# Copies of x in the places of late weights, an earlier DMA transpose of the third step's x, and stores placed behind a transpose

## The chip, the cores and the metric

The kernel runs on one core of one Trainium2 chip. The metric is the device time in microseconds (us) of that core.

TensorE is called PE in the views, VectorE DVE, ScalarE ACT, GpSimd POOL, SyncE SP. POOL issues the loads; SP issues stores and DMA transposes in the order of the program. Some words of the text: a transfer *lands* when its data are there and whoever waits for it may go on; the *chain* is the work that ended last, followed back step by step to what released it; an *eviction* is ACT's copy of a finished result out of PSUM; a *seed* is ACT's copy of a start value into the PSUM bank in which a part of a node is then summed; *dts* is a copy of one more sum of the node, from which DVE subtracts; *half clock* is a stretch in which the profile grants PE 0.50 of its clock.

## The reference

A causal convolution over time with eight taps, each a 512x512 matrix, on 8 sequences of 4096 steps.

```python
out = np.zeros_like(x)                       # x: [8, 4096, 512] float32
for k in range(8):
    shifted = x if k == 0 else np.concatenate([np.zeros((B, k, D)), x[:, :-k]], axis=1)
    out += np.matmul(shifted, kernel[k])     # kernel: [8, 512, 512]
```

## The kernel before

The kernel saves products with a Karatsuba-like scheme of three levels: for each pair of halves (LO, HI) of eight times and eight taps it also makes a middle one (MID), from sums of x and differences of weights. The sequence is cut into steps `i` of eight times for each of 128 partitions. A step has three nodes, LO, HI and MID, of nine products each (the very first node has 16 direct ones instead); a product is four matmuls of 128x512. The order of nodes is `(0,LO) (1,LO) (0,HI) (1,HI) (0,MID) (1,MID)`, then MID, LO, HI for each later step. Here "the second step" is `i = 1`, "the third" `i = 2`; node 6 is the first node of the third step. Up to node 6 every operation is placed by hand; from node 6 on there is a loop.

```python
def transpose_x(i, h):                       # DMA transpose, on SP
    nc.sync.dma_start_transpose(out=XT[:, 4*h:4*h+4, :]..., in_=xin[i, h]...)

def prep_m():                                # sums for the MID node of a step, on DVE
    tt(D1[:, 0:2], XT[:, 7::-7], XT[:, 0:2], ADD)
    tt(pairs(D2[:, 1:5]), pairs(XT)[:, 3::-3], pairs(XT)[:, 0:2], ADD)

def node_e(n, b_):                           # cut: nodes 4 and 5
    for a in (LO, HI):
        y = first[n.i, a, b_]
        tt(y, y, p, ADD if a == LO else SUB)
        store(n.i, a, b_, y)                 # on SP
...
# hand-placed part, around the second step's MID node (other lines cut)
tt(D1[:, 1], XT[:, 0], XT[:, 1], ADD)        # these sums read XT[0:4] of step 1
tt(D1[:, 0], X0[:, 1], XT[:, 0], ADD)
tt(D2[:, 1:3], X0, XT[:, 0:2], ADD)
tt(D2[:, 3:5], XT[:, 0:2], XT[:, 2:4], ADD)
node_u(nodes[5])                             # a product of XT[0] of step 1
prep_d21()
transpose_x(2, 0)                            # overwrites XT[0:4]
...
prep_m()                                     # first use of the third step's x
...
transpose_x(2, 1)                            # overwrites XT[4:8]
...
prep_d4(HI)                                  # the last sum before the loop
for k, (i, a) in enumerate(order):           # k >= 6
    if a == MID and more:
        transpose_x(i + 1, 0)                # for k == 6: "the third transpose"
```

`XT` is one buffer of eight times. A transpose of the next step can start only when every reader of the old contents is through. Below, `transpose_x(2, 0)` is the lower transpose, `transpose_x(2, 1)` the upper one and `transpose_x(3, 0)` the third.

## Time and profile before

| | before |
|---|---|
| median of the three runs known at the prediction | 787.44 us |
| span of the profiled run (its time: 786.55 us) | 784.4 us |
| PE, DVE, ACT busy | 98%, 84%, 36% |
| last sum before the loop ends | 88.3 us |
| node 8's first product of its last part starts | 100.75 us |

A line of a timeline has the start in us, the time taken, the engine, the line of the program, the operation, what it writes and reads, and how often it was repeated without a break. The bracket at its end is the idle time of the engine just before it, with what ended it. A loss "start to start" is the start of a line minus that of the line above, minus the number of matmuls in the line above times 0.2155 us.

The prediction shows PE and the chain. The timeline of DVE for the same hand-over, the stretch from about 68 to 101 us in which PE passes from the second step to the third, has three lines that matter:

```profile
69.43 0.70 DVE L76 TENSOR_TENSOR pp<-dts,pp 128x512 f32<-128x512 f32 x1 [0.82 <-ACT dts L276]
...
72.70 2.96 DVE L76 TENSOR_TENSOR D<-XT 128x1024 bf16<-128x1024 bf16 x3 [1.90 <-DMA XT<-xin]
...
87.09 1.23 DVE L76 TENSOR_TENSOR D<-XT 128x2048 bf16<-128x2048 bf16 x1 [0.50 <-DMA XT<-xin]
```

An engine that is behind with its list sits idle 0.82 + 1.90 + 0.50 = 3.2 us, 2.4 of them behind transposes. The line at 87.09 is the last sum, for which the third transpose must wait.

### The profile page before, as it was taken

The numbers are of one execution on the slowest core, as the hardware profiler recorded it, in microseconds if no ns is written. First come the engines' busy times: TensorE is split into PE (matmuls) and PEld (weight loads), VectorE is DVE, ScalarE is ACT, GpSimd is POOL, SyncE is SP. The second block draws the span as 40 slices with busy tenths as digits, with TensorE's granted clock in tenths as the row PEclk, the third lists the DMA queues.
The fourth block names the chain that finished last, engine by engine and source line by source line (L and its number), as shares of the span: only waits on it lengthen the run. The fifth ranks groups of instructions, "written<-read, shape, count | busy, mean of one in ns | idle before, by whom it ended". The sixth has DMA issues, their size and how long they took to land.

```text
span 784.4 us, 9508 instructions
## 1 busy us (share of the span) xinstructions
PE 767.3 (98%) x3620; PEld 349.0 (44%) x3620; DVE 659.3 (84%) x762; ACT 281.2 (36%) x458; POOL 42.8 (5%) x83
## 2 busy tenths in 40 slices
PE   7899999999999999999999999999999999999997
PEld 4444344444444444444444444444444444444443
DVE  3998898988888988888988888888888898888895
ACT  2363333233333333333333333333333333333332
POOL 5000000000000000000000000000000000000000
PEclk9999999999999999999999999999999999999999
DMA  9944987778778677978776888777778787788753
GB/s 164 210 76 118 259 187 164 190 174 170 191 185 197 163 183 167 190 177 206 165 192 162 172 195 198 171 178 173 175 172 204 186 169 179 166 177 199 177 154 125
DMA packets 159229, 138.37 MB, mean 176 GB/s; under 512 B 130130, under 2 KB 134226, under 8 KB 159184
## 3 DMA queue, kind: packets, MB, share of 16 engines
q1 hardware_dynamic: 145312, 98.84, 45.8%
q0 software_dynamic: 13728, 38.66, 30.6%
q8 instruction: 28, 0.46, 0.2%
q10 hardware_dynamic: 144, 0.26, 0.1%
q14 instruction: 17, 0.14, 0.1%
HBM read 77.32 MB, written 67.11 MB: 184 GB/s over the span
## 4 chain that ended last, share of the span: by engine, by line
PE 92%; DMA 5%; DVE 1%; POOL 1%; issue 0%; ACT 0%; DVEq 0%; SPq 0%; POOLq 0%
PE pp L214 91%; DMA XT<-xin 3%; DMA xin<-in_x_dram 2%; DVE D L76 1%; POOL w L80 0%; DVE y L76 0%; PE pp L191 0%; ACT XT L390 0%; POOL D L80 0%; DVE pp L76 0%; DVEq L629 0%; ACT pp L270 0%; POOL xin L80 0%; DVE f L76 0%; POOL identn L148 0%
## 5 line engine op out<-in xcount | busy, mean ns | idle before, releaser
L214 PE MATMUL pp<-w,D 128*128 128x512 bf16 x3304 | 721.6, 379 | 6.3 <-DVE pp L76 1.8
L214 PEld LDWEIGHTS <-D 128*128 128x128 bf16 x3304 | 322.6, 98 | 398.3 <-DVE D L76 5.4
L76 DVE TENSOR_TENSOR D<-D 128x1024 bf16<-128x1024 bf16 (+2 forms) x251 | 228.3, 949 | 0.1
L76 DVE TENSOR_TENSOR y<-pp,ms 128x1024 f32<-128x1024 f32 (+1 forms) x121 | 146.4, 1212 | 44.6 <-PE pp L214 44.5
L76 DVE TENSOR_TENSOR D<-XT 128x2048 bf16<-128x2048 bf16 (+2 forms) x155 | 143.4, 942 | 16.1 <-DMA XT<-xin 14.8
L258 ACT COPY pp<-pp 128x512 f32<-128x512 f32 x95 | 54.1, 570 | 261.5 <-PE pp L214 261.5
L270 ACT COPY pp<-pp 128x512 f32<-128x512 f32 x95 | 54.1, 570 | 170.6 <-PE pp L214 168.1
L76 DVE TENSOR_TENSOR pp<-dts,pp 128x512 f32<-128x512 f32 x95 | 65.6, 691 | 43.8 <-ACT dts L276 42.6
L314 ACT COPY ms<-pp 128x1024 f32<-128x1024 f32 x60 | 61.0, 1016 | 34.0 <-PE pp L214 34.0
L80 POOL DMA_DIRECT2D xin<-in_x_dram x64 | 34.0, 532 | 694.5 <-DMA XT<-xin 679.1
L286 DVE SCALAR_TENSOR_TENSOR pp<-pp,dts 128x512 f32<-128x512 f32 x95 | 66.0, 694 | 3.2
L276 ACT COPY dts<-pp 128x512 f32<-128x512 f32 x95 | 57.4, 604 | 2.0 <-PE pp L214 2.0
L272 ACT ACTIVATE pp<-pp 128x512 f32<-128x512 f32 x95 | 56.0, 589 | 1.9 <-DVE f L76 1.7
L214 PE MATMUL pp<-w,XT 128*128 128x512 bf16 x124 | 31.8, 379 | 0.0
L76 DVE TENSOR_TENSOR w<-w,w 128x2048 bf16<-128x2048 bf16 x19 | 22.6, 1217 | 3.2 <-DMA w<-in_kernel_dram 3.0
L214 PEld LDWEIGHTS <-XT 128*128 128x128 bf16 x124 | 12.1, 98 | 14.6
L185 PE MATMUL pp<-zero,ident 128*128 128x512 bf16 x20 | 6.6, 484 | 3.1 <-POOL ident masks.py:199 3.1
L214 PE MATMUL pp<-w,w 128*128 128x512 bf16 x36 | 8.6, 379 | 0.0
L356 DVE CAST D<-pp 128x1024 bf16<-128x1024 f32 x1 | 1.2, 1224 | 7.1 <-PE pp L202 7.1
L80 POOL DMA_DIRECT2D w<-in_kernel_dram x8 | 6.0, 768 | 1.9 <-DMA w<-in_kernel_dram 1.8
L191 PE MATMUL pp<-ident,xin 128*128 128x128 bf16 x48 | 3.2, 219 | 2.3 <-DMA xin<-in_x_dram 2.1
L214 PEld LDWEIGHTS <-w 128*128 128x128 bf16 x36 | 3.4, 98 | 3.8
(50 smaller groups left out, 68.7 us busy)
## 6 DMA issues: line engine op xcount, KB each, us to landing
out_dram<-y SPq DMA_DIRECT2D x123, 512.0 KB, 3.5
xin<-in_x_dram POOLq DMA_DIRECT2D x64, 512.0 KB, 5.7
w<-in_kernel_dram POOLq DMA_DIRECT2D x8, 512.0 KB, 16.5
out_dram<-ms SPq DMA_DIRECT2D x2, 512.0 KB, 3.3
out_dram<-f SPq DMA_DIRECT2D x2, 512.0 KB, 4.1
XT<-xin SPq DMA_TRANSPOSE x61, 6.2
D<-in_x_dram POOLq DMA_DIRECT2D x1, 508.0 KB, 5.5
D<-in_x_dram POOLq DMA_DIRECT2D x1, 381.0 KB, 7.0
```

The source lines that it names most:

```text
L76: nc.vector.tensor_tensor(out=o, in0=a, in1=b, op=op)
L80: nc.gpsimd.dma_start(out=out, in_=src)
L185: nc.tensor.matmul(pw[:, h], lhsT=ident, rhs=zero, start=True, stop=True)
L191: nc.tensor.transpose(o[:, t - t0, c * P:(c + 1) * P], src[:, t, c * P:(c + 1) * P], ident)
L214: nc.tensor.matmul(bank, lhsT=comp[:, c * P:(c + 1) * P], rhs=w[:, c, :], start=start and c == 0, stop=c == DC - 1, skip_group_check=True)
L258: nc.scalar.copy(out=n.q[:, 0], in_=n.q[:, 1])
L270: nc.scalar.copy(out=n.p[b_][:, 1], in_=n.q[:, 1])
L272: nc.scalar.mul(out=n.p[b_][:, 1], in_=n.q[:, 1], mul=-1.0)
L276: nc.scalar.copy(out=n.dts, in_=n.q[:, 0])
L286: nc.vector.scalar_tensor_tensor(out=p[:, 0], in0=p[:, 1], scalar=-1.0, in1=n.dts, op0=MUL, op1=SUB)
L314: nc.scalar.copy(out=ms[b_], in_=p)
L356: nc.vector.tensor_copy(out=D4[:, 0:2], in_=bank["d4a"])
```

## The change

Two places of weights that are filled late, `W[MID,HI,MID]` and `W[MID,LO,MID]`, hold copies of x until then: C1 the second step's first four times, C0 the first step's last two, which X0 held before. A tile of zeros takes a copy of one time (U1). The second step's middle sums A1 and D21 read the copies (F21 is made from D21), so the lower transpose can run long before. Moreover the additions of nodes 4 and 5 are parted from their stores, the stores come later (five of eight behind the upper transpose), and the whole hand-placed part, its start too, is in a new order. The diff, cut to its core:

```diff
-    X0 = spool.tile([P, 2, D], bf, name="X0")
+    A1 = spool.tile([P, 2, D], bf, name="A1")
+    U1 = zero
+        if (i, a) == (1, MID):
+            return (U1, [A1[:, 0], A1[:, 1]], [D21[:, 0], D21[:, 2]],
+                    [F21[:, j] for j in range(4)])
+    def node_y(n, b_, a):                    # addition without its store
+        y = first[n.i, a, b_]
+        tt(y, y, n.p[b_], ADD if a == LO else SUB)
+    C0, C1 = W[MID, HI, MID], W[MID, LO, MID]
# start: w4 first, transposes of H ahead, w6 before w5, another order of products
+    nc.scalar.copy(out=C0[:, 0:2], in_=XT[:, 6:8])
+    nc.scalar.copy(out=C1, in_=XT[:, 0:4])
# node 2
+    node_seed(nodes[2], 0)
+    nc.scalar.copy(out=U1, in_=XT[:, 0])
+    node_dts(nodes[2])
+    tt(A1[:, 0], C0[:, 1], C1[:, 0], ADD)
+    transpose_x(2, 0)
# nodes 3 and 4
+    tt(D21[:, 2:4], C1[:, 0:2], C1[:, 2:4], ADD)
+    tt(D21[:, 0:2], C0[:, 0:2], C1[:, 0:2], ADD)
+    tt(A1[:, 1], C1[:, 0], C1[:, 1], ADD)
+    prep_m()                                 # was ahead of node 5's last part
# nodes 5 and 6
+    prep_d4(LO)
+    store(0, LO, 1, first[0, LO, 1])
+    transpose_x(2, 1)
+    store(0, HI, 1, first[0, HI, 1])
+    node_y(nodes[5], 1, LO)                  # the tile ms
+    store(1, LO, 1, first[1, LO, 1])
```

More of the change, by code (lines that the diff above doesn't have):

```diff
@@ L306, in node_e @@
             first[n.i, n.a, b_] = y
-        elif n.k < 6:
-            for a in (LO, HI):
-                y = first[n.i, a, b_]
-                tt(y, y, p, ADD if a == LO else SUB)
-                store(n.i, a, b_, y)
         elif n.a == MID:
@@ L340, in direct @@
                 W[LO, n >> 1, n & 1], m == 0)
-    def add(y, p, op):
-        tt(y, y, p, op)
+    C0, C1 = W[MID, HI, MID], W[MID, LO, MID]
+    load_w(4)
+    transpose_pe("xh", 2, H, 5, 8)
+    sums_pe("d4a", 1, (-4, 0), (-3, 1))
     load(H[1:P, 1:4], xr[0:P - 1, RUN - 7:RUN - 4, :])
-    sums_pe("d4a", 0, (-4, 0), (-3, 1))
-    sums_pe("d4b", 3, (-2, 2), (-1, 3))
+    load_w(6)
+    sums_pe("d4b", 2, (-2, 2), (-1, 3))
+    nc.vector.tensor_copy(out=XF[:, 0:3], in_=bank["xh"])
     transpose_pe("xf", 2, xin[0, 0], 0, 4)
+    load_w(5)
@@ L353 @@
+    nc.vector.tensor_copy(out=D4[:, 0:2], in_=bank["d4a"])
     nc.scalar.copy(out=D4[:, 2:4], in_=bank["d4b"])
-    load_w(4)
     n0.p = {0: pair(0), 1: pair(1)}
-    nc.vector.tensor_copy(out=D4[:, 0:2], in_=bank["d4a"])
-    nc.scalar.copy(out=XF[:, 3:7], in_=bank["xf"])
-    transpose_pe("xh", 0, H, 5, 8)
-    direct(0, 2)
-    load_w(5)
-    load_w(6)
-    load_w(7)
-    load_x(0, 1)
-    direct(0, 3)
+    fill(pair(3))
+    load_w(7)
+    direct(0, 2)
+    direct(0, 1)
+    direct(0, 3)
@@ L365 @@
+    nc.scalar.copy(out=XF[:, 3:7], in_=bank["xf"])
     sums_pe("e4a", 2, (-5, -1), (-6, -2))
-    direct(0, 1)
-    nc.vector.tensor_copy(out=XF[:, 0:3], in_=bank["xh"])
     nc.vector.memset(XF[:, 0:3, 0:D:G], 0.0)
-    load_x(1, 0)
     tt(D2, XF[:, 0:5], XF[:, 2:7], ADD)
+    direct(2, 3)
+    tt(F21, D2[:, 0:4], D2[:, 1:5], ADD)
+    mid_dve(1, LO, HI)
+    sums_pe("e4b", 2, (-7, -3))
     direct(1, 2)
     direct(0, 0)
-    sums_pe("e4b", 2, (-7, -3))
-    tt(F21, D2[:, 0:4], D2[:, 1:5], ADD)
@@ L375 @@
-    mid_dve(1, LO, HI)
+    load_x(0, 1)
     tt(D1, XF[:, 2:4], XF[:, 3:5], ADD)
-    load_w(2)
+    mid_dve(2, LO, HI)
+    nc.scalar.copy(out=E4[:, 3:1:-1], in_=bank["e4a"])
+    mid_dve(2, LO, LO)
+    load_x(1, 0)
+    load_w(0)
     nc.vector.tensor_copy(out=E4[:, 1], in_=bank["e4b"][:, 0])
-    fill(pair(3))
-    mid_dve(1, LO, LO)
     direct(1, 3)
-    nc.scalar.copy(out=E4[:, 3:1:-1], in_=bank["e4a"])
-    nc.scalar.copy(out=F0, in_=XF[:, 3])
-    direct(2, 1)
-    mid_dve(2, LO, LO)
@@ L386 @@
-    mid_dve(2, LO, MID)
     direct(1, 1)
     transpose_pe("x1", 2, xin[0, 1], 0, 4)
-    mid_dve(2, LO, HI)
     nc.scalar.copy(out=XT[:, 4:8], in_=bank["x1"])
+    load_w(2)
+    mid_dve(1, LO, LO)
+    direct(1, 0)
+    transpose_pe("x2", 2, xin[1, 0], 0, 4)
+    mid_dve(2, LO, MID)
+    load_w(1)
+    tt(D4[:, 4:8], XF[:, 3:7], XT[:, 4:8], ADD)
+    direct(2, 1)
+    nc.vector.tensor_copy(out=XT[:, 2:4], in_=bank["x2"][:, 2:4])
+    prep_d42(HI)
+    nc.scalar.copy(out=XT[:, 0:2], in_=bank["x2"][:, 0:2])
@@ L391 @@
+    nc.scalar.copy(out=C0[:, 0:2], in_=XT[:, 6:8])
+    tt(T4, XT[:, 4:8], XT[:, 0:4], ADD)
     direct(3, 1)
-    tt(D4[:, 4:8], XF[:, 3:7], XT[:, 4:8], ADD)
-    direct(2, 3)
-    transpose_pe("x2", 2, xin[1, 0], 0, 4)
-    nc.scalar.copy(out=X0, in_=XT[:, 6:8])
+    prep_d41(HI)
+    tt(T42[:, 0:2], D4[:, 6:8], T4[:, 0:2], ADD)
+    direct(3, 0)
+    nc.scalar.copy(out=C1, in_=XT[:, 0:4])
     direct(2, 0)
-    nc.scalar.copy(out=XT[:, 0:2], in_=bank["x2"][:, 0:2])
-    prep_d42(HI)
-    direct(1, 0)
@@ L400 @@
-    direct(3, 0)
-    nc.vector.tensor_copy(out=XT[:, 2:4], in_=bank["x2"][:, 2:4])
-    tt(T4, XT[:, 4:8], XT[:, 0:4], ADD)
-    load_w(0)
-    load_w(1)
+    nc.scalar.copy(out=F0, in_=XF[:, 3])
     direct(3, 3)
+    fill(pair(2))
     tt(D41[:, 1], T4[:, 0], T4[:, 1], ADD)
-    fill(pair(2))
+    load_w(3)
+    tt(T42[:, 2:4], T4[:, 0:2], T4[:, 2:4], ADD)
     node_a1(1)
-    load_w(3)
-    tt(D41[:, 0], D4[:, 7], T4[:, 0], ADD)
-    mid_dve(1, HI, HI)
     direct(2, 2)
     node_e(nodes[0], 0)
+    tt(D41[:, 0], D4[:, 7], T4[:, 0], ADD)
@@ L414 @@
     node_a0(nodes[1])
+    node_u(nodes[1])
+    direct(3, 2)
+    mid_dve(1, HI, HI)
+    node_seed(nodes[1], 0)
     prep_d27()
-    node_u(nodes[1])
-    tt(T42[:, 2:4], T4[:, 0:2], T4[:, 2:4], ADD)
-    direct(3, 2)
-    tt(T42[:, 0:2], D4[:, 6:8], T4[:, 0:2], ADD)
+    node_dts(nodes[1])
+    node_seed(nodes[1], 1)
+    tt(D42[:, 3], D4[:, 1], D4[:, 3], ADD)
+    node_v(nodes[1], 0)
+    tt(D421[:, 0], D42[:, 7], T42[:, 0], ADD)
     load_x(1, 1)
-    tt(D42[:, 3], D4[:, 1], D4[:, 3], ADD)
@@ L422 @@
-    prep_d41(HI)
-    node_seed(nodes[1], 0)
+    node_v(nodes[1], 1)
+    tt(D421[:, 1:4], T42[:, 0:3], T42[:, 1:4], ADD)
+    node_a1(2)
+    mid_dve(2, HI, LO)
     transpose_x(1, 1)
-    node_dts(nodes[1])
-    node_v(nodes[1], 0)
-    node_seed(nodes[1], 1)
-    tt(D421[:, 0], D42[:, 7], T42[:, 0], ADD)
-    node_a1(2)
-    tt(D421[:, 1:4], T42[:, 0:3], T42[:, 1:4], ADD)
     mid_dve(1, HI, LO)
-    node_e(nodes[0], 1)
     node_d(nodes[1], 0)
-    node_v(nodes[1], 1)
-    mid_dve(2, HI, LO)
+    node_l(nodes[1], 0, LO)
@@ L436 @@
+    mid_dve(2, HI, MID)
     nc.scalar.copy(out=D4[:, 2:4], in_=T4[:, 2:4])
@@ L438 @@
     load_x(2, 1)
+    node_e(nodes[0], 1)
+    node_u(nodes[2])
     node_l(nodes[1], 0, HI)
-    node_l(nodes[1], 0, LO)
-    mid_dve(2, HI, MID)
     node_e(nodes[1], 0)
+    node_a0(nodes[2])
+    node_seed(nodes[2], 0)
     prep_d421(HI)
-    node_a0(nodes[2])
-    node_u(nodes[2])
+    load_x(2, 0)
     mid_dve(2, HI, HI)
+    node_l(nodes[1], 1, LO)
+    node_l(nodes[1], 1, HI)
+    nc.scalar.copy(out=U1, in_=XT[:, 0])
+    node_v(nodes[2], 0)
     prep_d4(HI)
-    node_seed(nodes[2], 0)
@@ L449 @@
-    node_l(nodes[1], 1, LO)
+    nc.scalar.copy(out=D42[:, 3], in_=T42[:, 3])
+    node_seed(nodes[2], 1)
+    node_v(nodes[2], 1)
     node_dts(nodes[2])
-    node_v(nodes[2], 0)
+    mid_dve(0, HI, HI)
+    node_e(nodes[1], 1)
+    prep_d41(HI)
     node_d(nodes[2], 0)
-    nc.scalar.copy(out=D42[:, 3], in_=T42[:, 3])
-    prep_d41(HI)
-    node_seed(nodes[2], 1)
-    node_l(nodes[1], 1, HI)
-    node_v(nodes[2], 1)
-    mid_dve(0, HI, HI)
+    node_l(nodes[2], 0, HI)
+    tt(A1[:, 0], C0[:, 1], C1[:, 0], ADD)
@@ L459 @@
+    prep_d42(HI)
     node_d(nodes[2], 1)
-    load_x(2, 0)
+    transpose_x(2, 0)
     mid_dve(0, LO, HI)
-    node_l(nodes[2], 0, HI)
-    node_e(nodes[1], 1)
     node_a1(3)
-    load_x(3, 0)
     node_l(nodes[2], 0, LO)
-    prep_d42(HI)
     node_a0(nodes[3])
     node_e(nodes[2], 0)
+    mid_dve(0, LO, LO)
+    tt(D421[:, 0:4], D42[:, 3:7], D42[:, 4:8], ADD)
     node_u(nodes[3])
+    node_l(nodes[2], 1, HI)
+    node_seed(nodes[3], 1)
+    node_seed(nodes[3], 0)
+    node_dts(nodes[3])
     mid_dve(1, MID, HI)
-    mid_dve(0, LO, LO)
@@ L473 @@
-    node_seed(nodes[3], 0)
-    node_seed(nodes[3], 1)
-    tt(D421[:, 0:4], D42[:, 3:7], D42[:, 4:8], ADD)
-    node_dts(nodes[3])
-    node_l(nodes[2], 1, HI)
+    node_v(nodes[3], 1)
+    node_d(nodes[3], 1)
+    mid_dve(0, HI, LO)
     node_v(nodes[3], 0)
+    node_d(nodes[3], 0)
+    node_l(nodes[2], 1, LO)
     node_a1(4)
-    node_v(nodes[3], 1)
-    node_d(nodes[3], 0)
-    mid_dve(0, HI, LO)
-    node_d(nodes[3], 1)
     mid_dve(1, MID, LO)
-    node_l(nodes[2], 1, LO)
+    tt(D21[:, 2:4], C1[:, 0:2], C1[:, 2:4], ADD)
@@ L486 @@
+    node_l(nodes[3], 1, HI)
+    node_l(nodes[3], 0, LO)
+    mid_dve(2, MID, MID)
+    node_e(nodes[2], 1)
+    load_x(3, 0)
     node_l(nodes[3], 0, HI)
-    node_e(nodes[2], 1)
-    node_l(nodes[3], 0, LO)
-    node_l(nodes[3], 1, LO)
     node_a0(nodes[4])
-    mid_dve(2, MID, MID)
+    tt(D21[:, 0:2], C0[:, 0:2], C1[:, 0:2], ADD)
     node_u(nodes[4])
     node_e(nodes[3], 0)
-    node_l(nodes[3], 1, HI)
+    node_l(nodes[3], 1, LO)
+    tt(A1[:, 1], C1[:, 0], C1[:, 1], ADD)
     mid_dve(2, MID, LO)
+    mid_dve(2, MID, HI)
@@ L496 @@
     node_seed(nodes[4], 0)
+    node_v(nodes[4], 0)
     node_seed(nodes[4], 1)
     node_dts(nodes[4])
-    mid_dve(2, MID, HI)
-    tt(D1[:, 1], XT[:, 0], XT[:, 1], ADD)
-    node_v(nodes[4], 0)
-    node_v(nodes[4], 1)
-    tt(D1[:, 0], X0[:, 1], XT[:, 0], ADD)
     node_d(nodes[4], 0)
     node_a1(5)
-    tt(D2[:, 1:3], X0, XT[:, 0:2], ADD)
+    node_v(nodes[4], 1)
+    prep_m()
+    node_l(nodes[4], 0, HI)
     node_l(nodes[4], 0, LO)
-    node_l(nodes[4], 0, HI)
-    tt(D2[:, 3:5], XT[:, 0:2], XT[:, 2:4], ADD)
@@ L510 @@
-    node_u(nodes[5])
-    node_d(nodes[4], 1)
     node_a0(nodes[5])
     node_e(nodes[3], 1)
+    node_d(nodes[4], 1)
+    node_u(nodes[5])
     node_seed(nodes[5], 0)
-    prep_d21()
+    node_l(nodes[4], 1, LO)
+    tt(F21[:, 0], D2[:, 0], D21[:, 0], ADD)
+    node_l(nodes[4], 1, HI)
+    node_y(nodes[4], 0, LO)
+    node_y(nodes[4], 0, HI)
+    store(0, LO, 0, first[0, LO, 0])
+    tt(F21[:, 1], D21[:, 0], D21[:, 1], ADD)
+    node_dts(nodes[5])
     node_v(nodes[5], 0)
+    prep_d27()
     node_seed(nodes[5], 1)
-    transpose_x(2, 0)
+    store(0, HI, 0, first[0, HI, 0])
@@ L519 @@
+    load_x(3, 1)
+    node_y(nodes[4], 1, LO)
     node_v(nodes[5], 1)
-    node_l(nodes[4], 1, LO)
-    node_e(nodes[4], 0)
-    node_l(nodes[4], 1, HI)
-    node_dts(nodes[5])
-    prep_d27()
     node_d(nodes[5], 0)
     node_d(nodes[5], 1)
-    prep_m()
+    tt(F21[:, 2:4], D21[:, 1:3], D21[:, 2:4], ADD)
     node_l(nodes[5], 0, LO)
@@ L530 @@
     node_a1(6)
+    node_l(nodes[5], 1, HI)
+    node_u(nodes[6])
     prep_d4(LO)
-    node_e(nodes[4], 1)
-    node_l(nodes[5], 1, HI)
+    store(0, LO, 1, first[0, LO, 1])
+    node_y(nodes[4], 1, HI)
     node_a0(nodes[6])
-    node_e(nodes[5], 0)
-    node_u(nodes[6])
+    node_y(nodes[5], 0, LO)
+    prep_d41(LO)
+    transpose_x(2, 1)
     node_l(nodes[5], 1, LO)
-    prep_d41(LO)
-    tt(D21[:, 2:4], D2[:, 2:4], D2[:, 3:5], ADD)
-    node_dts(nodes[6])
-    load_x(3, 1)
-    node_seed(nodes[6], 0)
-    tt(D21[:, 0:2], D2[:, 0:2], D2[:, 1:3], ADD)
-    node_seed(nodes[6], 1)
-    node_v(nodes[6], 0)
-    node_a1(7)
-    node_v(nodes[6], 1)
-    transpose_x(2, 1)
-    node_d(nodes[6], 0)
-    node_e(nodes[5], 1)
-    node_d(nodes[6], 1)
-    prep_d42(LO)
+    store(0, HI, 1, first[0, HI, 1])
+    node_seed(nodes[6], 0)
+    node_v(nodes[6], 0)
+    node_y(nodes[5], 0, HI)
+    tt(D21[:, 0:2], D2[:, 0:2], D2[:, 1:3], ADD)
+    node_dts(nodes[6])
+    node_seed(nodes[6], 1)
+    node_v(nodes[6], 1)
+    tt(D21[:, 2:4], D2[:, 2:4], D2[:, 3:5], ADD)
+    node_d(nodes[6], 0)
+    prep_d42(LO)
+    node_y(nodes[5], 1, HI)
+    node_d(nodes[6], 1)
+    store(1, LO, 0, first[1, LO, 0])
+    node_y(nodes[5], 1, LO)
+    store(1, HI, 0, first[1, HI, 0])
+    node_a1(7)
+    store(1, HI, 1, first[1, HI, 1])
     prep_d4(HI)
+    store(1, LO, 1, first[1, LO, 1])
     for k, (i, a) in enumerate(order):
```

## The prediction

> **What bounds the kernel now.** I read the page first, its table of engines and its chain that ended last.
>
> ```profile
> PE 767.3 (98%) x3620; PEld 349.0 (44%) x3620; DVE 659.3 (84%) x762; ACT 281.2 (36%) x458; POOL 42.8 (5%) x83
> ...
> PE 92%; DMA 5%; DVE 1%; POOL 1%; issue 0%; ACT 0%; DVEq 0%; SPq 0%; POOLq 0%
> ```
>
> TensorE (PE) is busy for 767.3 of 784.4 us, and 92% of the chain is PE. The change leaves every product in place (the same 866 products of four matmuls, the same transposes and fills), so only time in which PE waits can be won. Next, the windows: the stretch 200 to 400 us holds 928 matmuls, so a matmul costs 200/928 = 0.2155 us and a product of four 0.862 us. The kernel's steady part has no gap. The gaps are in the first 100 us, so I read the timeline of PE there.
>
> ```profile
> 22.08 1.03 PE L214 MATMUL pp<-w,D 128*128 128x512 bf16 x4
> 25.17 1.07 PE L191 MATMUL pp<-ident,xin 128*128 128x128 bf16 x16 [2.06 <-DMA xin<-in_x_dram]
> ...
> 68.18 1.89 PE L214 MATMUL pp<-w,D 128*128 128x512 bf16 x8 [0.71 <-ACT pp L270]
> ...
> 78.58 1.02 PE L214 MATMUL pp<-w,D 128*128 128x512 bf16 x4 [0.63 <-ACT pp L270]
> 80.85 8.87 PE L214 MATMUL pp<-w,D 128*128 128x512 bf16 x40 [1.25 <-ACT pp L272]
> 90.17 8.82 PE L214 MATMUL pp<-w,D 128*128 128x512 bf16 x40 [0.46 <-DVE D L76]
> 100.75 2.75 PE L214 MATMUL pp<-w,D 128*128 128x512 bf16 x12 [1.76 <-DVE pp L76]
> ```
>
> The idle in brackets is counted from the modelled end of the last matmul, so it is too small. Start to start it is more: 40 matmuls from 80.85 should take 8.62 us, until 89.47, and the next starts at 90.17: 0.70 lost. In the same way 0.88, 0.10, 0.80, 1.41, 0.70 and 1.96 us are lost at 68.18, 76.05, 78.58, 80.85, 90.17 and 100.75, together **5.85 us in the hand-over from the second step to the third**. Between 29 and 60 us some 0.7 us are lost, at 28.19 0.39, and at 25.17 2.23 in the wait for the second half of the first x. The loop after 100.75 loses nothing.
>
> What ends those late waits is in the chain in order of time: ACT and VectorE (DVE) are only the last links, behind three DMA transposes.
>
> ```profile
> 66.68 6.00 DMA XT<-xin
> 72.67 0.02 issue
> 72.70 2.96 DVE D L76 x3
> ...
> 80.65 6.34 DMA XT<-xin
> ...
> 88.39 8.72 DMA XT<-xin
> 97.11 0.02 issue
> ```
>
> The first transpose (third step, lower half) can start at 66.68 only: XT[0:4] is read until then by the second step's sums D1, D2 and by a product of XT[0]. DVE sits until 72.70. The second one (upper half) waits behind DVE work and a store until 80.65; the third (fourth step, lower half) waits for the last sum of the third step, at 88.3, and the sums behind it at 97.1 feed the product at 100.75. So DVE is late through all of it.
>
> **What the Trainium skill says.** "TensorE: Matmul & The Clock Gate", section "Wait — 56ns, not 53.3ns?", gives 215.7 ns start to start for 512 columns at the full clock; the trace agrees (215.5). "VectorE: DVE Perf Modes", section on the perf-mode tiers, gives 1224 ns for a 2048-element bf16 tensor_tensor; the trace has 1217 as the duration. Back to back such operations start 1.135 us apart here (42.65, 43.79, 44.92), and I count with that. "Perfetto Trace Analysis", on HWDGE instructions, says that an issue's window leaves out the movement of the data: agreed, the issue at 80.65 shows 4.75 us on the SP queue and lands after 6.34. "DMA: Bandwidth & Descriptors", rules for authors, advises to issue a transfer early and wait late. That is what this change does.
>
> **The change, part by part.**
>
> *Copies.* X0 goes (one 1024-element ACT copy, 1.05 us). C0 takes its place (1.05), and C1 (2048 elements, 1.87 by the like copy at 26.27) and U1 (512, 0.62 by the F0 copy) are added on ACT: +2.5 us on an engine that is half idle between 28 and 45 us. In a place where ACT waited for PE 3.8 us (before 34.11) C1 costs nothing. They free XT[0:4] when prep_d4(HI) has read it, by my count at 46 us instead of 66.7. The lower transpose is then bound by its input: that load is issued at 45.15 now, lands in about 5.7, so transpose from about 51 to 57 us, in a stretch where the DMA engines show a share of 0.00. It leaves the path: **prep_m wants it only at about 64**.
>
> *DVE.* Spacings from the DVE timeline: 2048 bf16 1.135 us, 1024 0.60, 512 0.335, a float32 addition of 1024 from PSUM 1.13, a 512 subtraction in PSUM 0.60. The second step's middle sums were 0.335x2 + 0.60x2 + 1.135 = 3.0; they become A1 0.335x2, D21 0.60x2 and F21 0.335x2 + 0.60 = 3.14. All else moves. From 28.15 on I add DVE's list in its new order, to the last sum before the loop: weights' differences done by 63.2, then 21.2 us more, plus some 0.65 of waits where PE delivers late (the y of node 4's second half): **85.0**, against 88.3 before. DVE, not PE, now sets this date.
>
> *PE.* The same 8 direct products stand before the transposes of the second half of x; that half is the eighth or so transfer, and the same bytes lie ahead of it in the queue (order w4, H, w6, w5, w7 instead of H, w4, w5, w6, w7). So it lands at 25.1 as before and the 2.23 us stay, though the first product may come some 0.4 us sooner; that only lengthens this wait. Then one product instead of two lies beside the 1.87 us eviction, 0.86 us more of waiting up to 28.19. From 29.05: 58 products and one fill to the first product of node 6's last part: 58 x 0.862 + 0.43 = 50.4, with some 0.6 of small waits for DVE: 80.1. Before this product started at 82.57. **Won there: 2.5 us.**
>
> *What remains.* In the loop PE would reach node 8's first last-part product at 80.1 + 18 products x 0.862 = 95.6; before it was 100.75. But this product hangs on the third transpose: last sum 85.0, transpose 6.2 (median landing) to 8.7 (its time now), then prep_m, a sum and a subtraction, 3.6 us as now (97.11 to 100.75): 94.9 to 97.4. With a middle value of 7.6 for the transpose it is 96.3, so 0.7 us of the 5.1 stay. Sum: 100.75 - 96.3 = **4.4 us won**, and all later times move by it. 787.44 - 4.4 = 783.0.
>
> *Stores behind transposes.* The adds are split from their stores, and the stores stand later in the SP queue. This frees the transpose of the upper half at about 74 (prep_d4(LO) done) instead of 80.65. It lands near 80.5, before DVE wants it at 84.
>
> **The rivals.**
>
> 1. *A wait of stores takes the place of the transposes.* The tile ms is written again by node 6's eviction on ACT, which must wait for the second step's store. That store now stands behind the upper transpose, whose issue holds SP for some 4.75 us from 74: store at 79.5, landing (3.3 in the table of issues, more behind a transpose) at 83 to 84.7. PE delivers at 82. ACT then seeds node 7 at 84.6 to 86.2, and PE wants that at 84.5: 0 to 1.8 us lost. Against: the product at 96.3 is set by DVE and the third transpose, so a loss here is mostly hidden behind the one already counted. It would make 783 to 784.5.
>
> 2. *DVE is the bound, and nearly all stays.* From 30 to 60 us DVE is busy 9.93, 10.00 and 9.96 of each 10 us. If the new order leaves it a wait (a weight late, the eviction of x), each microsecond goes into the last sum and the third transpose. With 2 us of such waits 785.
>
> 3. *The start moves too.* If the w4-first order and the transposes of H beside the wait for x let everything begin earlier, up to 2.6 us at 25.17 and 28.19 are to be had: 780.5. Against: the DMA share is 1.19 from 10 to 20 us, the queue is saturated, and the awaited transfer has the same bytes ahead of it.
>
> 4. *The transposes were hidden anyway*, and nothing comes of it: 787. Against it are the 5.85 us of counted gaps, which the chain puts behind exactly these transposes.
>
> **Range and chances.** Best: all 5.85 and a little of the start, 781.0. Worst plausible: half of the hand-over regained by DVE waits and stores, 785.6. I put 783.0 in the middle. Faster by over 2% would need 15.7 us; all gaps after the first product are 9.2 us, so next to impossible. Slower by 2% would need a new wait in every step of the loop, and the loop's text is untouched.
>
> **What would show it.** Right: PE's timeline without gaps of over 0.5 us from 30 to 85; the lower transpose issued near 51; no DVE wait for XT near 70; the upper one issued near 74; the third near 85, and one residual gap of 0 to 1.7 us near 96; the first half of x still awaited until about 25. Wrong: x landing well before 24 (rival 3); ACT's ms eviction waiting for a store (rival 1); the last sum before the loop later than 86.5 (rival 2); or new gaps inside the loop after 105, which would mean that the order of x loads shifted against the transposes there.

## The result, and the profile after

Over six runs each, the changed kernel takes 783.22 us in the median (782.97 to 784.06), the kernel before 787.81 (786.40 to 789.12). The ratio is 0.9945, with a 95% interval from 0.9932 to 0.9958. A ratio is the mean time of one kernel's runs over that of the other's of the same rounds, so it is not quite the ratio of the medians. The two profiled spans are 784.4 and 780.9 us, 3.5 us apart.

The page's engines and chain after:

```profile
PE 767.4 (98%) x3620; PEld 349.0 (45%) x3620; DVE 659.3 (84%) x764; ACT 283.2 (36%) x460; POOL 42.8 (5%) x83
...
PE 94%; DMA 3%; DVE 1%; POOL 1%; issue 0%; ACT 0%; DVEq 0%; POOLq 0%
```

Nothing has become less work: PE and DVE are as busy as before, ACT has 2.0 us more. Only the DMA's part of the chain fell, from 5% to 3%. PE's timeline after, at the lines that answer to those in the prediction:

```profile
20.07 3.61 PE L215 MATMUL pp<-w,D 128*128 128x512 bf16 x16 [0.91 <-DMA w<-in_kernel_dram]
25.08 1.07 PE L192 MATMUL pp<-ident,xin 128*128 128x128 bf16 x16 [1.40 <-DMA xin<-in_x_dram]
...
28.10 1.05 PE L192 MATMUL pp<-ident,xin 128*128 128x128 bf16 x16 [1.09 <-ACT XT L390]
...
39.95 8.10 PE L215 MATMUL pp<-w,D 128*128 128x512 bf16 x36
48.79 12.28 PE L215 MATMUL pp<-w,D 128*128 128x512 bf16 x56 [0.74 <-DVE pp L76]
...
70.58 1.89 PE L215 MATMUL pp<-w,D 128*128 128x512 bf16 x8
72.66 1.89 PE L215 MATMUL pp<-w,F 128*128 128x512 bf16 x8 [0.19 <-DVE pp L76]
...
78.71 21.32 PE L215 MATMUL pp<-w,D 128*128 128x512 bf16 x96
99.86 1.03 PE L215 MATMUL pp<-w,XT 128*128 128x512 bf16 x4
```

- The large gaps from 68 to 101 us are gone. Start to start, 0.36 us are lost at 72.66 (70.58 + 8 x 0.2155 = 72.30), 0.46 between 78.71 and 99.86, 0.18 at 63.67: 1.0 us in place of 5.85. **The hand-over won 4.85 us.**
- A new gap stands at 48.79: 39.95 + 36 x 0.2155 = 47.71, so 1.08 us. With two small ones the stretch from 29 to 60 us loses 1.25 us in place of 0.7. **0.55 us are given back.**
- In the start, the second transposes on PE begin at 28.10 in place of 28.19, but one product fewer (0.862) is done by then: **0.77 us given back.** x still arrives at 25.08.

4.85 - 0.55 - 0.77 = 3.53, the difference of the spans. The chain after, in order of time, shows what is left of the hand-over:

```profile
72.66 13.27 PE pp L215 x61
85.93 7.70 DMA XT<-xin
93.63 0.02 issue
93.66 1.01 DVE D L76 x2
```

One transpose is left in this stretch of the chain, the third. DVE's timeline shows where its idle time went:

```profile
64.54 0.69 DVE L76 TENSOR_TENSOR D<-XT 128x1024 bf16<-128x1024 bf16 x1
65.60 1.23 DVE L76 TENSOR_TENSOR D<-XT 128x2048 bf16<-128x2048 bf16 x1 [0.37 <-PE pp L215]
...
84.64 1.22 DVE L76 TENSOR_TENSOR D<-XT 128x2048 bf16<-128x2048 bf16 x1
```

The first two lines are prep_m, which stood at 72.70 before, behind the lower transpose. The third is the last sum, 2.45 us earlier than at 87.09 and without a wait.

### The profile page after: what moved, and what is told of

Its sections match the earlier page's. It is cut to its first block, busy times and chain, and to the rows that moved or that the text cites. A ratio compares the mean times of both kernels' runs of the same rounds, so it can differ in the third digit from the quotient of the medians.

```text
span 780.9 us, 9507 instructions
## 1 busy us (share of the span) xinstructions
PE 767.4 (98%) x3620; PEld 349.0 (45%) x3620; DVE 659.3 (84%) x764; ACT 283.2 (36%) x460; POOL 42.8 (5%) x83
## 3 DMA queue, kind: packets, MB, share of 16 engines
q1 hardware_dynamic: 145312, 98.84, 46.3%
## 4 chain that ended last, share of the span: by engine, by line
PE 94%; DMA 3%; DVE 1%; POOL 1%; issue 0%; ACT 0%; DVEq 0%; POOLq 0%
PE pp L215 94%; DMA xin<-in_x_dram 2%; DMA XT<-xin 1%; POOL w L80 0%; DVE D L76 0%; PE pp L192 0%; DVE pp L76 0%; ACT XT L390 0%; DVE y L76 0%; POOL D L80 0%; DVEq L648 0%; POOL xin L80 0%; POOL identn L148 0%; PE pp L186 0%; POOL ident masks.py:199 0%
## 5 line engine op out<-in xcount | busy, mean ns | idle before, releaser
L76 DVE TENSOR_TENSOR D<-D 128x2048 bf16<-128x2048 bf16 (+2 forms) x250 | 227.2, 948 | 3.4 <-ACT D L369 3.4
L215 PE MATMUL pp<-w,F 128*128 128x512 bf16 x36 | 8.7, 379 | 0.2 <-DVE pp L76 0.2
```

The lines of the kernel that those rows point to most:

```text
L76: nc.vector.tensor_tensor(out=o, in0=a, in1=b, op=op)
L215: nc.tensor.matmul(bank, lhsT=comp[:, c * P:(c + 1) * P], rhs=w[:, c, :], start=start and c == 0, stop=c == DC - 1, skip_group_check=True)
```

## The experiments

In each batch all kernels ran on one chip with runs of the kernel before between them. The changed kernel itself was run again in the second and third batch, so three ratios of it are known: 0.9945, 0.9957 and 0.9949.

### Was it the early transpose? One copy undone

```diff
-            return (U1, [A1[:, 0], A1[:, 1]], ...
+            return (XT[:, 0], [A1[:, 0], A1[:, 1]], ...
-    nc.scalar.copy(out=U1, in_=XT[:, 0])
-    transpose_x(2, 0)                        # node 2
     node_u(nodes[5])
+    transpose_x(2, 0)
     tt(F21[:, 2:4], D21[:, 1:3], D21[:, 2:4], ADD)
+    prep_m()                                 # was in node 4
```

> The changed kernel with one copy undone: the second step's middle stream is read from XT[0] and not from U1, so the lower transpose (third step) must again wait for that product (about 68.8 us), and prep_m follows it, just ahead of node 6. Theory (the gain is the early lower transpose): transpose issued near 69, lands near 75, DVE waits for it about 1 us and does prep_m late, last sum before the loop near 88, product of node 8 near 99.9 instead of 97.3; span up by 2 to 3 us over the changed kernel's 780.9, ratio to before 0.997 to 0.999. Rival (the gain comes from the reordered start and stores, copies only accompany it): span within 1 us of 780.9, ratio 0.994 to 0.996.

Measured: 788.35 us (787.18 to 788.99), ratio 1.0015 (1.0003 to 1.0027), span 786.6. The whole gain is gone and a little more. The direction fits the theory and contradicts the rival; the size does not: the span is 5.7 us above 780.9, twice what was expected. DVE hardly waited for the lower transpose. The last sum came about as expected, started at 86.85 (84.64 in the changed kernel; 0.5 us of that is x landing later in this run). What was not expected is in the chain:

```profile
85.72 1.22 DVE ms L76
86.94 0.02 issue
86.96 10.19 DMA out_dram<-ms
97.15 0.02 issue
97.17 1.02 ACT ms L317
```

The second step's second store of ms took 10.19 us to land, next to the third transpose, which was issued at 88.14 and landed at 99.0, after 10.8 us (7.7 in the changed kernel). ACT's eviction into ms waited for it, and PE for ACT: 1.79 us are lost start to start at 98.84. The first store of ms did the same a little earlier. It stands behind the upper transpose, whose issue held SP for 5.93 us from 77.17 (1.70 in the changed kernel), so it went out at 83.77 only; ACT waited 3.39 us for it, until 87.74, and PE lost 1.46 us at 89.29. That is the prediction's rival 1, here as it was written. The cause of the long issue and the long landings stays open. A load of x issued shortly before was my suspicion, since this kernel's loads wait for its transposes (74.44 and 85.74, against 55.59 and 79.78 in the changed one); but where the upper transpose here, issued 2.7 us behind such a load, took 8.0 us to land, that of the stores-only kernel below, issued 2.5 us behind one, took 4.7.

### Was it the early sums? prep_m alone moved back

```diff
     node_v(nodes[4], 1)
-    prep_m()
     tt(F21[:, 2:4], D21[:, 1:3], D21[:, 2:4], ADD)
+    prep_m()
```

> The changed kernel with only the third step's first sums (prep_m, 1.74 us of DVE) moved back from node 4 to just ahead of node 6's first product; copies, early lower transpose and all else as changed. Theory (what gains is that this DVE work falls into DVE's waits for PE near 65 us): DVE idles about 2 us near 65 to 68, last sum near 87.5 instead of 85.8, the upper transpose later by as much, ratio 0.998 to 1.001, much as where U1 was not copied. Rival (what gains is that nobody waits for the lower transpose): within 0.7 us of the changed kernel.

Measured: 784.89 us, ratio 0.9973 (0.9959 to 0.9986); the changed kernel on the same chip 783.86, ratio 0.9957. The five times of the one (784.59 to 785.80) and of the other (783.71 to 784.06) do not overlap. So the early sums are worth about 1.0 us of the gain: less than the theory claimed, more than the rival allowed. DVE idles as foretold:

```profile
65.22 0.70 DVE L290 SCALAR_TENSOR_TENSOR pp<-pp,dts 128x512 f32<-128x512 f32 x1 [0.96 <-PE pp L215]
66.95 0.43 DVE L76 TENSOR_TENSOR F<-D,D 128x512 bf16<-128x512 bf16 x1 [1.03 <-PE pp L215]
```

This kernel and the one above do the same sums at the same place, behind the same products; they differ in U1 and in when the lower transpose runs, at 50 or 69 us. By their ratios they are 0.0042 x 787 = 3.3 us apart (they ran on different chips, and each ratio is known to about 1 us). That is what the early transpose is worth beyond the sums in this order of stores. It does not reach the time by DVE's wait for XT: DVE's operations follow each other in the same way in both traces, 0.85 us later in the one with U1 not copied, down to the last sum (86.00 and 86.85). What differs is how long SP is held and how late stores and transposes land: the two waits for stores of ms told of above.

### The copies in the old order

The kernel before with C0, C1, U1, the sums from them and the early lower transpose, everything else as it was:

```diff
-    nc.scalar.copy(out=X0, in_=XT[:, 6:8])
+    nc.scalar.copy(out=C0[:, 0:2], in_=XT[:, 6:8])
+    nc.scalar.copy(out=C1, in_=XT[:, 0:4])
+    nc.scalar.copy(out=U1, in_=XT[:, 0])
     load_x(2, 0)
+    transpose_x(2, 0)
+    # A1 and D21 (four sums) just ahead of mid_dve(2, MID, LO); D1 and D2 of step 1 removed
-    prep_d21()
-    transpose_x(2, 0)
+    # F21 in two sums
```

> The kernel before with only the copies (C0, C1, U1), the middle sums made from them, and the lower transpose moved up behind the load of its input; start, stores and the rest of the order as before. Theory (the copies carry nearly all): lower transpose near 51, no DVE wait for XT near 70, last sum near 86.3 instead of 88.3, node 8's product near 97.7 instead of 100.75; 3 us gained, ratio 0.995 to 0.997. Rival (the new order of start and stores is needed for the gain): under 1.2 us gained, ratio above 0.998.

Measured: 786.81 us, ratio 0.9998 (0.9985 to 1.0011), and a wrong result (relative error 0.18): my F21 was written while node 4 still had to read it. No gain. Two reasons are in the trace. My four sums stood ahead of a weight difference that PE wanted at once, which cost PE two waits, and in this execution PE ran at half clock from about 25.6 to 29.0 us (more on that below):

```profile
63.62 1.04 PE L215 MATMUL pp<-w,D 128*128 128x512 bf16 x4 [1.11 <-DVE w L76]
64.84 1.02 PE L215 MATMUL pp<-w,D 128*128 128x512 bf16 x4 [0.19 <-DVE w L76]
```

The second try spread these sums and moved prep_m as the changed kernel has them, and gave a correct result:

```diff
+    tt(A1[:, 0], C0[:, 1], C1[:, 0], ADD)              # node 2
     mid_dve(1, MID, LO)
+    tt(D21[:, 2:4], C1[:, 0:2], C1[:, 2:4], ADD)
     mid_dve(2, MID, MID)
+    tt(D21[:, 0:2], C0[:, 0:2], C1[:, 0:2], ADD)
+    tt(A1[:, 1], C1[:, 0], C1[:, 1], ADD)
     node_d(nodes[4], 0)
+    prep_m()
     node_l(nodes[4], 1, HI)
+    tt(F21[:, 2:4], D21[:, 1:3], D21[:, 2:4], ADD)
```

> The kernel before with the copies and the early lower transpose (as in the kernel that gave a wrong result, now without overwriting F21 too early) and, new, the third step's sums D1 and D2 and the second step's sums moved to the places that they have in the changed kernel; start and stores as before. Theory now (the gain is DVE work moved from behind the transposes into time in which DVE waited for PE, the copies only allow it): last sum before the loop near 86.5, node 8's product near 98.3, 2 to 3 us gained, ratio 0.996 to 0.9975, if no half-clock stretch falls into the profile. Rival (the start's and the stores' new order are needed): like the copies alone, under 1 us.

Measured: 787.94 us, ratio 1.0012 (0.9999 to 1.0026). The theory missed again:

```profile
74.72 0.69 DVE L76 TENSOR_TENSOR F<-D 128x1024 bf16<-128x1024 bf16 x1 [3.45 <-PE pp L215]
```

The sum of F21 must wait for node 4's last product, which in the old order of PE comes late; DVE is held for 3.45 us in front of subtractions that PE needs, and PE then waits 1.72 us itself. A half-clock stretch, which the expectation had excepted, is in this trace too, from about 26.6 to 30 us. In both traces the place of a sum costs PE waits; that these ate the whole gain is likely and not shown. The two tries show that the copies bring nothing without an order of PE and DVE that fits; they do not show that no such order exists near the old one.

### The stores

The changed kernel with the stores back behind their additions, and the kernel before with only the stores moved:

```diff
 def node_y(n, b_, a):                        # changed kernel, stores inline
     tt(y, y, n.p[b_], ADD if a == LO else SUB)
+    store(n.i, a, b_, y)                     # and the eight later stores removed
```

> The changed kernel with each store of nodes 4 and 5 put right behind its addition again, so that three of them stand ahead of the upper transpose on SP. Theory (the order of the stores is worth little): the upper transpose is issued near 77.8 instead of 74.96, lands near 84, just when DVE wants it at 84.6; span within 0.6 us of 780.9, and ACT's wait for a store of ms (1.94 us at 91.92) shrinks. Rival (the store order carries a good part of the gain): DVE waits 1 us or more for XT near 85 and the span rises by 1 to 2 us.

```diff
             tt(y, y, p, ADD if a == LO else SUB)        # kernel before
-            store(n.i, a, b_, y)
+    store(0, LO, 0, ...); store(0, HI, 0, ...)         # behind node 4's first additions
+    transpose_x(2, 1)                                  # now ahead of prep_d41(LO)
+    store(0, LO, 1, ...); ...                          # the other six behind it
```

> The kernel before with only the stores of nodes 4 and 5 parted from their additions and six of the eight put behind or later than the upper transpose; no copies. Theory: the upper transpose is issued near 75.7 instead of 80.65, which takes away only the 0.5 us for which DVE waits for it at 87; at most 0.6 us gained, ratio 0.999 to 1.0. Rival (SP's queue was what held the hand-over): 1.5 us or more gained, ratio 0.998 or less.

Measured: 783.93 us, ratio 0.9957 (0.9945 to 0.9969) with the stores inline, which is inside the changed kernel's own three ratios; and 786.61 us, ratio 0.9998 (0.9986 to 1.0010), for the stores alone in the kernel before. Neither shows a worth of the stores' order, as the theory had it. The profiled span with the stores inline, 782.2, is 1.3 us above 780.9 where the theory allowed 0.6; but DVE does not wait for XT near 85, which was to be the rival's mark, and the changed kernel's own spans go up to 781.9. The trace of the stores-only kernel is of its slowest run (788.82, with a long stretch of half clock), so its dates cannot be compared with those expected. (With the stores inline five of them stand ahead of the upper transpose, not three as the expectation says.) One detail of the first expectation fell: ACT's wait for the store of ms did not shrink; that store, issued at 85.32 and landing after 7.66 us, is in this kernel's chain.

### The start, and PE's clock

The expectation for the next run came from a surprise: in two of the three traces that had the old start, PE's clock was halved behind the wait for x. The windows of the stores-only kernel (stretch, its length, then busy us and instructions of PE, PEld, DVE, ACT and POOL, granted clock, DMA share, GB/s):

```profile
26.00:28.00 2.00, 1.73 (x17) 1.74 (x18) 2.00 (x3) 0.00 (x0) 0.00 (x0) 0.50 1.17 200
28.00:30.00 2.00, 2.00 (x7) 0.69 (x5) 0.43 (x1) 1.81 (x1) 0.54 (x1) 0.50 1.24 206
30.00:32.00 2.00, 2.00 (x10) 1.08 (x9) 1.88 (x2) 1.10 (x2) 0.00 (x0) 0.50 1.24 205
```

At 0.50 a 512-column matmul takes 0.43 us start to start. The page before shows no such stretch. So I filled the wait in the kernel before:

```diff
+    wf = pair(2)
+    for _ in range(4):
+        fill(wf)                             # two matmuls on zeros each
     transpose_pe("x1", 2, xin[0, 1], 0, 4)
```

> The kernel before with eight more matmuls on zeros in front of the transposes of the second half of x, in the 2.2 us in which PE waits for it: some 1.7 us of work beside the wait. Theory (after this wait PE runs at half clock for some microseconds in part of the executions, as in two of the three traces with the old start, and that is what spreads the times of before from 786.1 to 789.1): no half clock in the trace, spread under 1 us, median near 786.3, ratio 0.998 to 0.9995. Rival (the spread has another source, DMA for one): median and spread like before's, ratio 0.9995 to 1.0005.

Measured: 785.81 us, ratio 0.9984 (0.9971 to 0.9996): four runs within 785.46 to 785.89 and one at 787.23, the only one of the five with a mean clock of 0.996. The trace has no half clock. So eight useless matmuls make the kernel before faster by 0.16%; the ratio is as expected, the median 0.5 us lower, and the spread of 1.8 us, by the one slow run, is wider than the 1 us expected. The runs of the kernel before fit: over the three batches, the 14 with a mean clock of 0.997 or less average 787.63 us, the 12 with 0.999 or 1.000 average 786.87. The clock is thus likely one source of its spread, not the only one. A mean clock is a rough sign, though: in the changed kernel's first trace (0.998) the only half clock is from 778.4 us on, 2.0 us after PE's last matmul, where it costs PE nothing. Of the traces kept, the three with half clock near 26 us have 0.996 or 0.997, the others 0.998 to 1.000.

The converse, the changed kernel with the old start:

```diff
-    load_w(4)
-    transpose_pe("xh", 2, H, 5, 8)
-    ...                                      # the changed start, to the transposes "x2"
+    load(H[1:P, 1:4], ...)
+    sums_pe("d4a", 0, (-4, 0), (-3, 1))
+    ...                                      # the start of before
+    direct(1, 0)                             # left over from it; direct(2,1), (3,1) taken out
```

> The changed kernel with the start of before (order of loads, preparation and first ten direct products up to the transposes of x's third half); the rest as changed. Theory (the new start is worth nothing in a trace without half clock, it even costs 0.6 us of waits, but it takes away the half-clock stretch behind the wait for x): runs spread over 2 us or more, some with a clock of 0.998 or less, median 0.5 to 1.5 us above the changed kernel; fastest run no slower than the changed kernel's. Rival (the start is neutral): median within 0.3 us of the changed kernel and spread under 0.7 us.

> The changed kernel once more, as the base on this chip for the three others: ratio to before 0.994 to 0.9965, clock 0.999 or above in every run.

Measured: 784.19 us (783.43 to 784.77), ratio 0.9957, three of five runs with a clock of 0.997 or 0.998; the changed kernel beside it 783.39 us (783.11 to 783.74), ratio 0.9949. The medians are 0.8 us apart as the theory had it, and the spread is twice as wide, though not 2 us; the ratios' intervals overlap, and the fastest run is 0.3 us slower than the changed kernel's, where the theory had it no slower. The changed kernel's clock missed its expectation too: not 0.999 or above in every run, but 0.998 in three of five (in the trace of one of them all half clock lies behind PE's last matmul). The trace of the old start shows no half clock but a longer wait for x (2.84 us of idle, x at 25.98) and a new gap of 0.77 us at 34.70, so I cannot say how much of the 0.8 us is the clock.

The base of the second batch was run with this expectation and gave 783.86 us, 0.9957 (0.9945 to 0.9970):

> The changed kernel itself, for a second trace and for runs on the same chip as the three others: ratio to before 0.994 to 0.997, span 780 to 782.5.

### What is left: two tries to better the changed kernel

```diff
     node_seed(nodes[2], 0)
+    node_dts(nodes[2])
-    nc.scalar.copy(out=U1, in_=XT[:, 0])
-    nc.scalar.copy(out=D42[:, 3], in_=T42[:, 3])
     node_seed(nodes[2], 1)
+    nc.scalar.copy(out=U1, in_=XT[:, 0])
+    nc.scalar.copy(out=D42[:, 3], in_=T42[:, 3])
-    node_dts(nodes[2])
-    prep_d41(HI)
     node_d(nodes[2], 0)
+    prep_d41(HI)
```

> The changed kernel with one thing mended in node 2: ACT copies dts right behind the first seed, ahead of U1 and the copy of D42, and DVE subtracts (node_d) before prep_d41. Theory (the gap of about 0.9 us at 48.8, where the prediction counted 0.25, is ACT's new U1 copy and DVE's order ahead of the subtraction): gap 0.4 us or less there, time 0.2 to 0.6 us lower. Rival (the gap is the late upper transpose of the second step, on which the sum before it waits 0.5 us): gap stays above 0.7 us.

The lines of PE around the gap, first of the changed kernel on that chip, then of this one:

```profile
43.67 4.26 PE L215 MATMUL pp<-w,D 128*128 128x512 bf16 x19
48.81 3.41 PE L215 MATMUL pp<-w,D 128*128 128x512 bf16 x15 [0.88 <-DVE pp L76]
```

```profile
43.79 8.43 PE L215 MATMUL pp<-w,D 128*128 128x512 bf16 x37
```

The gap shrank from 1.05 us start to start to 0.27 (at 48.38), so the order of operations there was its main cause, as the theory had it; which part of it is told below. The time did not move: 783.68 us, ratio 0.9952, against 783.39 and 0.9949. The second half of the theory, that the gap was worth its length, fell. DVE starts its sum on the second step's upper transpose at 45.36 in place of 45.19 and works almost without a break until the last sum, which starts at 84.84 in place of 84.66. What PE gained is given back in later waits, among them 0.27 us at 60.79 and 0.48 at 62.99 in place of 0.18.

```diff
+    direct(2, 1)                             # besides the edit above
     transpose_pe("x2", 2, xin[1, 0], 0, 4)
-    node_y(nodes[5], 1, HI)                  # f
+    node_y(nodes[5], 1, LO)                  # ms
     ...
     prep_d4(HI)
+    node_y(nodes[5], 1, HI)
+            if k == 6: store(1, HI, 1, first[1, HI, 1])   # behind the third transpose
```

> As the kernel before this in the list, and with direct(2,1) ahead of the transposes that wait for the eviction (fills 0.86 of 1.25 us at 28), and with the addition and store of the second step's ms ahead of the last sum and of f, so that the third transpose starts some 1.1 us earlier and ACT's eviction no longer waits for the store of ms. Theory (DVE's list up to the last sum and the transpose behind it set the end of the hand-over): third transpose near 84.5, node 8's product near 96.2, 0.8 to 1.3 us under the changed kernel. Rival (PE waits elsewhere take its place, for one at node 7's seed, which now waits for the last addition): under 0.4 us.

Measured: 783.63 us, ratio 0.9952. The third transpose did start earlier, at 84.93 in place of 85.95, and ACT no longer waits for the store of ms. The rival took the gain:

```profile
86.70 3.61 PE L215 MATMUL pp<-w,D 128*128 128x512 bf16 x15 [0.71 <-ACT pp L274]
```

Node 7's seed waits for the addition that now comes last, and PE for the seed (0.96 us start to start). No version beat the changed kernel.

## Why the prediction was right

The time was 783.0 predicted, 783.22 measured. By its own steps:

- **The bound.** Right. The gaps of the hand-over were the only place with a gain; 4.85 of the 5.85 us went, and the loop did not change.
- **x's arrival.** Right: 25.1 predicted, 25.08 found. The 0.86 us more of waiting at the eviction are there too: 1.26 in place of 0.39 start to start at 28.10.
- **The lower transpose.** Predicted from about 51 to 57, found issued at 50.75 and landed after 4.3 us, with the next load released by it at 55.59. The upper one: 74 predicted, 74.96 found.
- **The last sum, the third transpose, node 8's product.** Predicted 85.0, 7.6 us and 96.3; found 85.8, 7.70 us and 97.28. So the traces show a gain of 3.5 us where the sum said 4.4.
- **The term that was mis-sized** is DVE's date, "weights' differences done by 63.2, then 21.2 us more, plus some 0.65 of waits [...]: **85.0**". These differences were done at 63.8 and the last sum at 85.8, and the product that hangs on it comes 0.98 us later than 96.3, nearly all of it from this date: the third transpose is issued at 85.93 and takes 7.70 us where 7.6 were counted. Up to 63.2 the list has no wait for the second step's upper transpose, and there is one, of 0.52 us, in the first line here (the last line is ACT's, the others DVE's):

```profile
45.17 1.23 DVE L76 TENSOR_TENSOR D<-XT 128x2048 bf16<-128x2048 bf16 x1 [0.52 <-DMA XT<-xin]
46.31 1.22 DVE L76 TENSOR_TENSOR w<-w,w 128x2048 bf16<-128x2048 bf16 x1
47.45 0.69 DVE L76 TENSOR_TENSOR D<-D 128x1024 bf16<-128x1024 bf16 x1
48.05 0.69 DVE L76 TENSOR_TENSOR pp<-dts,pp 128x512 f32<-128x512 f32 x1
...
46.75 0.58 ACT L280 COPY dts<-pp 128x512 f32<-128x512 f32 x1
```

- **PE's date was mis-sized too**, and it did not count. "58 x 0.862 + 0.43 = 50.4, with some 0.6 of small waits for DVE: 80.1 [...] Won there: 2.5 us": the product came at 81.3 (78.71 + 12 x 0.2155), so 1.3 us were won. I had allowed 0.25 us for node 2 within that 0.6; it cost 1.08. The lines above show why: DVE's subtraction for node 2, the fourth line, stands behind the late sum of the first line, a difference of weights and one more sum of 0.60 us, and DVE works through these without a break. ACT's new copy U1 is not the cause, though the expectation of the experiment with dts named it: dts was ready at 47.33, before DVE got to it, and with U1 not copied the same gap stays (0.89 us at 49.26). That experiment moved both dts and the subtraction and took most of the gap away, by these lines because of the subtraction; it shows that it was worth nothing in the end: the date that counts is DVE's, and there the 0.50 us of wait for the transpose stayed.
- **Slips in its sums, without effect.** The program has 871 products, not 866: the 20 matmuls on tiles named F were left out of the count. 85.0 + 7.6 + 3.64 is 96.2, not 96.3. The worst case of 785.6 does not follow from its words: half of 4.4 or of 5.85 us lost again gives 785.2 or 785.9.
- **Why the time fits all the same.** The profiled execution of before was one of its quickest, 786.55 us; its median over six runs is 787.81. The medians differ by 4.6 us, the traces by 3.5. Part of what is between them may be the half clock, which was seen near 26 us in some traces with the old start and in none with the new one: none of the 16 timed runs of the changed kernel has a mean clock below 0.998, while 14 of 29 of the kernel before do. The prediction did not see this; its sum promised 0.9 us more than the traces gave, so its good fit to the medians is partly luck.
- **Rival 1 (the store of ms)** was no loss in the changed kernel, but only by a hair. ACT does wait there:

```profile
91.92 1.01 ACT L317 COPY ms<-pp 128x1024 f32<-128x1024 f32 x1 [1.94 <-DMA out_dram<-ms]
```

It is the second ms store, not the first one that the prediction looked at, and behind it PE lost 0.11 us start to start, at 93.59. In five of the variants this store lies in the chain, and with U1 not copied both stores of ms together are the main part of the loss.
- **Rival 2** (DVE as the bound) came half true: 0.8 us of the last sum. **Rival 3** (an earlier start) is refuted; the wait for x stays. **Rival 4** (hidden anyway) is refuted by the gain itself, and by the copy undone, which loses all of it.
- **How the gain comes about** was only half understood. I put it down to DVE's waits for XT. The experiments give about 1.0 us to the early sums and about 3.3 us to the early transpose itself, because SP is held for less long and transposes and stores land sooner; the start is worth some 0.8 us by medians whose ratios' intervals overlap, and nothing is measurable for the stores. These shares are what is lost when one part is taken out of the changed kernel. They come from different kernels and batches and need not add up to the gain; put into the old order, the copies and the early transpose gained nothing.

## What to carry to other kernels

When an engine that is behind waits for a transfer, count what its whole list gains when the transfer comes early, and then look at which stores, loads and evictions share the queue and the buffers with it. Before a gap is blamed on a new copy, look whether the engine that needs the result was free to use it: here it was not, and the copy cost nothing that the traces show. A closed gap on the busiest engine is worth nothing while another engine's list sets the date. Compare medians with the clock of each run: one trace can be the quick one.

## What the Trainium skill lacked or had wrong

- "TensorE: Matmul & The Clock Gate", section "What's actually happening", has the clock halve after at least one idle window of about 3.4 us. Here a wait of 2.17 us start to start, in the first try of the copies, was followed by half clock from about 25.6 to 29.0 us; with the old start in the changed kernel a wait of 3.00 us was not. And at the end of the changed kernel's trace the clock halves 2.0 us after PE's last matmul (776.35 to 778.4). So half clock also came after a wait shorter than that window, in some executions only. What decides it no run here shows.
- "Advanced Engine Details and Errata", section "X-Bar Transpose (TRN2)", says that such transposes are as fast as regular DMAs, at 350 to 400 GB/s. Here one of 512 KB (128x2048 bf16, SBUF to SBUF) took 4.3 us from its issue at 50.75 to landing, with hardly anything else on the DMA engines: 524288 bytes in 4.3 us are 122 GB/s, and no 1-us window of it shows more than 215 GB/s. A store of 512 KB lands in 3.4 us in the median, a transpose in 6.1.
- No page that I read says how long a store or a transpose takes when both run together; here the store of ms took 7.2 to 10.2 us in several variants, against 3.3 in the median in the kernel before.
